# Head sums and means as float32r pairs, sample states as weights once, and a shorter lead, in a one-core hybrid decoder step

## The chip, the cores and the metric

The kernel runs on one core of a Trainium2 chip. The time is the device time of one execution in microseconds. Before the change, three runs took 1477.34, 1478.21 and 1481.64 us; the median is 1478.21.

A core has five engines that run side by side, each with its own instruction queue taken in order: TensorE (PE, matrix products; its weight loads are shown apart as PEld), VectorE (DVE), ScalarE (ACT), GpSimd (POOL) and SyncE (SP, which issues most of the transfers here). Products land in PSUM, in banks of 512 float32 columns; the other engines read them from there.

## The reference

One decoder layer runs for 512 prompt tokens and for 8 requests of 8 new tokens each, with shared weights; the kernel puts both beside each other as 576 columns. The layer is a half-step SwiGLU network, then three branches in parallel (an RWKV-7 recurrence, a causal convolution, attention to 256 memory tokens) that are gated and merged, then another SwiGLU network. The change touches three places of the recurrence. Cut down, they are:

```
s  = s * w_t + (s @ -kk_t) kka_t^T + v_t k_t^T ;  o_t = s @ r_t      # state per head, 64 x 64
mean = o.mean(-1);  var = square(o - mean).mean(-1)                  # per head of 64
o  = (o - mean) * rsqrt(var + GN_EPS) * gn_g + gn_b
o  = o + sum(r_h * k_h * r_k, -1) * v_h                              # head sum
```

The prompt starts with a state of zero; each of the 8 requests starts with its own state, an input. The new states are outputs.

## The kernel before

Data lie with channels on the 128 partitions and tokens along the columns, in halves of 288. A weight product in full precision is made of three float32r products: each operand is split into a high part (rounded to float32r, by a copy on ScalarE) and a low part (the rest, by a subtraction on VectorE), and high x high, high x low and low x high are added (`split`, L95; `mm3k`, L108). Smaller products outside the weight matrices are plain float32, which the instruction stream shows as two instructions each.

The program has a first SwiGLU network (to about 420 us), the mixing part (to about 985 us), the merge and the second network. The mixing part follows a written list of steps, `PLAN` (L28). For each of four pairs of heads there are `prep` (P: decays, keys, the 64-token products), `inverse` and `joined` (I, J: a triangular inverse, on VectorE and by transfers) and `chain` (B). The letters X, Y and Z are gate steps: large weight products that are independent of the chains.

The order on each engine is not the order of the text. A planner places instructions by its own estimate of when their data are ready, the earlier step of the program first, and so fills TensorE's gaps in a chain with weight products (L110) of later steps. A few products are pinned in program order (`busy` and parts of `chunks`). Once placed, the order on an engine is fixed.

*Head sums.* `prep` forms `k` = r k r_k on VectorE (L876). `full` (L122) multiplies it by `bd`, the 128 x 128 matrix with ones in the two 64 x 64 diagonal blocks, and L880 multiplies that sum by `v` to give `bv`.

*Chain.* `chain` transposes keys and values, runs `chunks` (L1041), eight steps of 64 prompt tokens that each need the state left by the one before, then `sample_chunk` (L1077) for the 64 sample tokens, then the normalisation. In `sample_chunk`, `ms` holds the 8 requests' states, loaded from `wst` by SyncE, as 128 x 128 blocks with two heads on the diagonal. They enter twice: L1086 lets them move against the weights `ax`, which hold request b's 8 columns of the decayed key and zeros elsewhere, and L1091 takes them as weights for the 8 columns of the receptance. L1098 to L1100 form the state's increment, with two buffers named "u2", and L1103 and L1104 update the states on VectorE before they are stored.

*Means.* L921 to L927 multiply the chain's output by `cen`, the identity minus the mean within a head, copy the result to `rs` and square it on ScalarE. Sums of squares, a root, a reciprocal and the rest follow; the last step of the fourth chain splits `ya` for the merge.

*Lead.* The program begins with 16 empty products on zeros (L207, `busy`), while the first half of the first slice of `x`, the vector table `pv`, and then slices of weights and of `x` by turns come in on SyncE's queue (L208 to L220).

Of the kernel before, what the change touches and what calls it, by code (L numbers as in the profile page):

```python
# [6 lines left out]
F32 = mybir.dt.float32  # L7
F32R = mybir.dt.float32r
AF = mybir.ActivationFunctionType
# [7 lines left out]
NB = 8  # L17
TS = 8
N = SEQ + NB * TS
H = N // 2  # L20
# [26 lines left out]
def _q8(t, q):  # L47
    return t.rearrange("p (b q) -> p b q", q=q)


class _Builder:
# [13 lines left out]
    def con(self, name, w=128):  # L65
        return self.cst[:, _CC[name]:_CC[name] + w]
# [107 lines left out]
    def build(self):  # L174
        tc, a = self.tc, self.a
        with ExitStack() as st:
# [19 lines left out]
            with ExitStack() as sf:  # L196
# [7 lines left out]
                x = [x1p.tile([128, N], F32, name=f"x{k}") for k in range(8)]  # L204
                idle = fp.tile([128, H], F32, name="m1")[:, :128]
                self.G.memset(idle, 0.0)
                self.busy(idle, idle, 16)  # L207
                self.dma(x[0][:, :H], a["x"][:, 0, :H])  # L208
                self.dma(self.pv, a["pv"])
                raw = []  # L210
# [3 lines left out]
                for k in range(8):  # L214
                    if k:
                        self.dma(x[k], a["x"][:, k, :])
                    self.dma(raw[k].rearrange("p (j c) -> p j c", j=3),
                             a["wu1"][:3, :, 128 * k:128 * (k + 1)].rearrange("j p c -> p j c"))
                    if not k:
                        self.dma(x[0][:, H:], a["x"][:, 0, H:])  # L220
                self.dma(self.cst, a["cst"])
# [3 lines left out]
                c = _COLS["mu"]  # L225
                self.V.tensor_scalar(self.omu, self.pv[:, c:c + 15], -1.0, 1.0, ALU.mult, ALU.add)
                c = _COLS["ka"]
# [22 lines left out]
            for step in PLAN.split():  # L250
                n = int(step[1:])
# [31 lines left out]
            x = [x2p.tile([128, N], F32, name=f"x2{k}") for k in range(8)]  # L283
# [321 lines left out]
    def lora(self, lp):  # L605
# [18 lines left out]
        self.ms = lp.tile([128, NB, 128], F32, name="ms")  # L624
        self.ax = lp.tile([128, 9, 64], F32, name="ax")
        for t in self.z:
            self.G.memset(t[:, 0:1], 0.0)
        self.G.memset(self.gi, 0.0)
        for t in self.padded(self.gi):
            self.G.memset(t[:, :, 0:1], 1.0)  # L630
        for t in self.st + [self.ms, self.ax]:
            self.G.memset(t, 0.0)
# [179 lines left out]
    def prep(self, j):  # L812
# [65 lines left out]
        bv = tmp("bv", 2)  # L878
        for c, p in self.full("g", (bd, k)):
            V.tensor_tensor(bv[:, c], p, v[:, c], ALU.mult)  # L880
# [17 lines left out]
    def chain(self, j):  # L898
# [21 lines left out]

        sq, rs = (b3.tile([128, 640], F32, name="u2", bufs=2)[:, :N] for _ in range(2))  # L921
        for c0, c1 in ((0, 5), (5, 9)):
            c = slice(64 * c0, 64 * c1)
            p = self.bank("c")[:, :64 * (c1 - c0)]
            T.matmul(_q8(p, 64), con("cen"), ra[:, c0:c1, 0, :], start=True, stop=True)
            A.copy(rs[:, c], p)
            A.activation(sq[:, c], rs[:, c], AF.Square)  # L927
        p = self.sums("c", [sq], con("bd")[:, ::64], slice(0, N))
# [148 lines left out]
    def sample_chunk(self, j, gr, kbt, vu, ra, gc):  # L1077
        V, A, T = self.V, self.A, self.T
        b3 = self.b3
        ms, ax = self.ms, self.ax  # L1080
        for h in range(2):
            s = slice(64 * h, 64 * h + 64)
            self.dma(ms[s, :, s], self.a["wst"][j, s])
        A.copy(_q8(ax.rearrange("p b t -> p (b t)"), 72)[:, :, :8], _q8(ra[:, 8, 1, :], 8))
        ps = self.values(8, gr, vu)
        self.solve(8, gr, vu, ps, [(ax[:, b, :], ms[:, b, :]) for b in range(NB)])  # L1086
        for h in range(2):
            s = slice(64 * h, 64 * h + 64)
            T.matmul(ps[s, 384:448], vu[:, 8, s], gr[:, h, 8, :64], start=True, stop=False)
        for b in range(NB):  # L1090
            T.matmul(ps[:, 384 + 8 * b:392 + 8 * b], ms[:, b, :], ra[:, 8, 0, 8 * b:8 * b + 8], start=False,  # L1091
                     stop=b == NB - 1)
        A.copy(ra[:, 8, 0, :], ps[:, 384:448])
# [169 lines left out]
```

## Time and profile before

| What | Value |
|---|---|
| Median of three runs | 1478.21 us |
| Profiled execution, its own time | 1475.84 us |
| Its span in the profile | 1474.1 us |
| TensorE busy | 1456.3 us (99%) |
| TensorE weight loads busy | 1376.0 us (93%) |
| VectorE busy | 1027.2 us (70%) |
| ScalarE busy | 674.3 us (46%) |
| HBM traffic | 97 GB/s over the span |

Products overlap in TensorE's pipeline and their ends are modelled, so a busy share of 99% does not say that every one runs at its peak pace. A line of a group reads: source line, engine, operation, output and inputs with shapes, count, then busy time and mean duration in ns, then idle time before it and what ended it. The chain of waits follows the work back from the last instruction, at each step to what released it. The granted clock is a share of TensorE's full clock.

### The profile page before, as it was taken

Reading aid. Unit: us, or ns where it says so; the run is one execution under the profiler, and the core shown is the slowest. Engines: PE = TensorE matmul, PEld = TensorE weight load, DVE = VectorE, ACT = ScalarE, POOL = GpSimd, SP = SyncE. Lnnn points to the kernel's source line nnn. Section 1 sums busy time; section 2 is a strip of 40 time slices with the busy share of each in tenths; the row PEclk is TensorE's granted clock in tenths of the full one; section 3 lists DMA queues with packets and bytes.
Section 4 is the critical chain, followed back from the end, with each engine's and each line's share of the span. In section 5 each row is a group of like instructions: output and inputs, shape, how many; then the busy total and the mean of one; then the engine's idle time right before and its main releaser. Section 6 shows DMA issues by size and latency. Waiting matters only on the chain.

```text
span 1474.1 us, 27109 instructions
## 1 busy us (share of the span) xinstructions
PE 1456.3 (99%) x10820; PEld 1376.0 (93%) x10820; DVE 1027.2 (70%) x2054; ACT 674.3 (46%) x1371; POOL 4.7 (0%) x22
## 2 busy tenths in 40 slices
PE   9999999999999999999999999999999999999998
PEld 9999999999999798889888888889999999999997
DVE  7976777777794579769456556357588667777765
ACT  7443434444577545435446543444354334344342
POOL 0000000000010000000000000000000000000000
PEclk9999999999999999999999999999999999999999
DMA  6222222223632144123223124355322322322221
GB/s 211 72 83 90 87 86 87 86 86 106 205 106 86 49 149 92 47 80 103 55 67 114 55 85 139 92 188 169 103 72 72 100 86 73 104 95 89 86 87 65
DMA packets 95178, 144.06 MB, mean 98 GB/s; under 512 B 43644, under 2 KB 53500, under 8 KB 95052
## 3 DMA queue, kind: packets, MB, share of 16 engines
q1 hardware_dynamic: 94476, 141.74, 31.5%
q8 instruction: 85, 1.39, 0.4%
q10 hardware_dynamic: 576, 0.59, 0.1%
q14 instruction: 41, 0.34, 0.1%
HBM read 126.07 MB, written 16.23 MB: 97 GB/s over the span
## 4 chain that ended last, share of the span: by engine, by line
PE 92%; DVE 4%; ACT 1%; DMA 1%; issue 1%; SPq 0%; DVEq 0%; ACTq 0%
PE p L110 51%; PE p L382 26%; PE c L1033 1%; PE g L893 1%; PE c L1037 1%; PE c L1023 1%; DVE pr L986 1%; PE c L128 1%; PE g L1056 1%; DVE cc L676 1%; PE g L128 1%; PE g L1054 1%; PE c L1050 1%; DMA w<-win 1%; PE c L1091 1%
## 5 line engine op out<-in xcount | busy, mean ns | idle before, releaser
L110 PE MATMUL p<-x,wh 128*128 128x288 f32 x3136 | 650.8, 299 | 1.4 <-ACT kv L562 0.7
L110 PEld LDWEIGHTS p<-x,wh 128*128 128x128 f32 x3136 | 504.4, 188 | 14.7 <-issue 7.4
L110 PE MATMUL p<-x,wl 128*128 128x288 f32 x1568 | 467.4, 298 | 2.3 <-DVE wl L97 2.1
L96 ACT CAST wh<-w 128x512 fp32r<-128x512 f32 (+1 forms) x353 | 209.9, 600 | 256.1 <-PE p L382 99.9
L97 DVE TENSOR_TENSOR wl<-w,wh 128x512 fp32r<-128x512 f32 (+1 forms) x353 | 232.0, 662 | 129.6 <-ACT wh L96 124.1
L110 PEld LDWEIGHTS p<-x,wl 128*128 128x128 f32 x1568 | 294.0, 188 | 7.1 <-DVE wl L97 2.7
L382 PE MATMUL p<-t,wh 128*128 128x288 f32 x1088 | 224.4, 299 | 0.0
L382 PEld LDWEIGHTS p<-t,wh 128*128 128x128 f32 x1088 | 173.8, 188 | 6.4 <-DVE t L393 6.4
L382 PE MATMUL p<-b,wh 128*128 128x288 f32 x816 | 169.7, 295 | 0.0
L382 PE MATMUL p<-t,wl 128*128 128x288 f32 x544 | 160.5, 295 | 0.0
L96 ACT CAST wh<-p 128x512 fp32r<-128x512 f32 x136 | 84.5, 621 | 155.9 <-PE p L110 117.3
L382 PEld LDWEIGHTS p<-b,wh 128*128 128x128 f32 x816 | 132.7, 188 | 0.0
L97 DVE TENSOR_TENSOR wl<-p,wh 128x512 fp32r<-128x512 f32 x136 | 93.7, 689 | 50.5 <-ACT wh L96 47.8
L382 PE MATMUL p<-b,wl 128*128 128x288 f32 x408 | 120.3, 295 | 0.0
L382 PEld LDWEIGHTS p<-t,wl 128*128 128x128 f32 x544 | 102.4, 188 | 0.0
L382 PEld LDWEIGHTS p<-b,wl 128*128 128x128 f32 x408 | 76.8, 188 | 0.0
L460 DVE SCALAR_TENSOR_TENSOR x<-p,x 128x288 f32<-128x288 f32 x128 | 57.9, 452 | 19.9 <-PE p L110 19.9
L96 ACT CAST x<-t 128x576 fp32r<-128x576 f32 (+1 forms) x60 | 36.5, 610 | 45.7 <-DVE t L464 42.5
L372 DVE TENSOR_TENSOR p<-w 128x512 f32<-128x512 f32 x68 | 46.7, 687 | 4.6 <-DMA w<-wu 4.2
L372 DVE TENSOR_TENSOR p<-p,w 128x512 f32<-128x512 f32 x68 | 46.5, 683 | 0.3 <-DMA w<-wu 0.2
L1067 DVE SCALAR_TENSOR_TENSOR st<-c,gc,mg 64x64 f32<-64x64 f32 x56 | 15.9, 283 | 42.8 <-PE c L1050 42.1
L676 DVE SCALAR_TENSOR_TENSOR cc<-up,pv,cc 128x512 f32<-128x512 f32 x60 | 43.5, 743 | 0.2
(354 smaller groups left out, 1979.4 us busy)
## 6 DMA issues: line engine op xcount, KB each, us to landing
w<-wu SPq DMA_DIRECT2D x85, 512.0 KB
w<-win SPq DMA_DIRECT2D x44, 512.0 KB
w<-wd SPq DMA_DIRECT2D x64, 256.0 KB
w<-wd SPq DMA_DIRECT2D x16, 384.0 KB
d_mb<-gate SPq DMA_DIRECT2D x16, 288.0 KB
w<-wo SPq DMA_DIRECT2D x8, 512.0 KB
d_x<-x SPq DMA_DIRECT2D x16, 144.0 KB
d_g<-gate SPq DMA_DIRECT2D x8, 288.0 KB
```

Source lines behind the costliest of these rows:

```text
L96: self.A.copy(hi, x)
L97: self.V.tensor_tensor(lo, x, hi.bitcast(F32), ALU.subtract)
L110: self.T.matmul(p, l, x[r][:, c], start=k == 0 and i == 0, stop=k == n - 1 and i == 2)
L128: self.T.matmul(p, l, r[:, c], start=i == 0, stop=i == len(ops) - 1)
L372: V.tensor_tensor(s, u, v, ALU.add)
L382: self.T.matmul(p, hl[l][:, c], xs[k][b][:, o], start=first and k == 0 and q == 0, stop=k == 3 and q == 2, skip_group_check=True)
L460: V.scalar_tensor_tensor(x[m][:, c], p, 0.5, x[m][:, c], ALU.mult, ALU.add)
L676: V.scalar_tensor_tensor(c[:, :SEQ], up[:, k:k + SEQ], w, c[:, :SEQ], ALU.mult, ALU.add)
L893: T.matmul(ps[:, i * 128:(i + 1) * 128], kb[o, c + i].rearrange("p a t -> p (a t)"), ra[o, c + i].rearrange("p a t -> p (a t)"), start=Tru ...
L986: V.tensor_tensor(pr, tt[:, :n, :e].unsqueeze(2).broadcast_to([np_, n, m, e]), l3[:, t:e, :e].unsqueeze(1).broadcast_to([np_, n, m, e]), A ...
L1023: p = self.T.matmul(ps[64:, 64 * h:64 * h + 64], gr[:64, h, c, 64:], vu[:64, c, 64 * h:64 * h + 64], start=h == 0 or alone, stop=alone)
L1067: V.scalar_tensor_tensor(mn[s, s], ps[s, 256 + 64 * h:320 + 64 * h], gc[s, c:c + 1], mg[s, s], ALU.mult, ALU.add)
```

## The change

- The head sums in `prep` become two float32r products: `k` is split into `kh` and `kl`, in the buffers "av" and "u1", and both are multiplied by `bdr`, a float32r copy of `bd`. The copy is exact, since the matrix holds ones and zeros.
- The centring in `chain` does the same with `cenr`, a float32r copy of `cen`, whose entries (63/64, -1/64 and 0) are exact too. The output is split into `yh` and `yl`, in "u2" buffers. Both banks are filled before they are copied to `rs`, and the square is one instruction over all columns. The two casts are made once, in `lora`.
- In `sample_chunk` the states are weights once: one product for each request moves 16 columns, 8 of the receptance and 8 of the key, into a bank "g" that is copied to `am`. Two identity products then add the halves where the old products added theirs. `ax` is gone.
- In the lead, 10 empty products stand in place of 16, and the first slice of weights is issued ahead of the first half of `x` and of `pv`.

```diff
-                self.busy(idle, idle, 16)
-                self.dma(x[0][:, :H], a["x"][:, 0, :H])
-                self.dma(self.pv, a["pv"])
+                self.busy(idle, idle, 10)
...
                     if not k:
+                        self.dma(x[0][:, :H], a["x"][:, 0, :H])
+                        self.dma(self.pv, a["pv"])
                         self.dma(x[0][:, H:], a["x"][:, 0, H:])
...
-        self.ax = lp.tile([128, 9, 64], F32, name="ax")
+        self.bdr, self.cenr = (lp.tile([128, 128], F32R, name=n) for n in ("bdr", "cenr"))
+        self.A.copy(self.bdr, self.con("bd"))
+        self.A.copy(self.cenr, self.con("cen"))
...
-        for c, p in self.full("g", (bd, k)):
+        kh = b1.tile([128, N], F32R, name="av")
+        kl = b1.tile([128, 640], F32R, name="u1", bufs=2)[:, :N]
+        self.split(kh, kl, k)
+        for c, p in self.full("g", (self.bdr, kh), (self.bdr, kl)):
...
-        sq, rs = (b3.tile([128, 640], F32, name="u2", bufs=2)[:, :N] for _ in range(2))
+        yh, yl = (b3.tile([128, 640], F32R, name="u2", bufs=2)[:, :N].rearrange("p (c t) -> p c t", t=64) for _ in "hl")
+        self.split(yh, yl, ra[:, :, 0, :])
+        cen = []
         for c0, c1 in ((0, 5), (5, 9)):
-            c = slice(64 * c0, 64 * c1)
-            p = self.bank("c")[:, :64 * (c1 - c0)]
-            T.matmul(_q8(p, 64), con("cen"), ra[:, c0:c1, 0, :], start=True, stop=True)
+            cen.append((slice(64 * c0, 64 * c1), self.bank("c")[:, :64 * (c1 - c0)]))
+            for i, y in enumerate((yh, yl)):
+                T.matmul(_q8(cen[-1][1], 64), self.cenr, y[:, c0:c1], start=i == 0, stop=i == 1)
+        rs = b3.tile([128, 640], F32, name="u2", bufs=2)[:, :N]
+        for c, p in cen:
             A.copy(rs[:, c], p)
-            A.activation(sq[:, c], rs[:, c], AF.Square)
+        sq = b3.tile([128, 640], F32, name="u2", bufs=2)[:, :N]
+        A.activation(sq, rs, AF.Square)
...
-        A.copy(_q8(ax.rearrange("p b t -> p (b t)"), 72)[:, :, :8], _q8(ra[:, 8, 1, :], 8))
+        q = self.bank("g")[:, :128].rearrange("p (b i t) -> p b i t", b=NB, i=2)
+        for b in range(NB):
+            T.matmul(q[:, b], ms[:, b, :], ra[:, 8, :, 8 * b:8 * b + 8], start=True, stop=True)
+        am = b3.tile([128, 2, 64], F32, name="am")
+        A.copy(am.rearrange("p i (b t) -> p b i t", t=8), q)
         ps = self.values(8, gr, vu)
-        self.solve(8, gr, vu, ps, [(ax[:, b, :], ms[:, b, :]) for b in range(NB)])
+        self.solve(8, gr, vu, ps, [(am[:, 1], ident)])
...
-        for b in range(NB):
-            T.matmul(ps[:, 384 + 8 * b:392 + 8 * b], ms[:, b, :], ra[:, 8, 0, 8 * b:8 * b + 8], start=False,
-                     stop=b == NB - 1)
+        T.matmul(ps[:, 384:448], ident, am[:, 0], start=False, stop=True)
```

More of the change, by code (lines that the diff above doesn't have):

```diff
@@ L630, in lora @@
             self.G.memset(t[:, :, 0:1], 1.0)
-        for t in self.st + [self.ms, self.ax]:
+        for t in self.st + [self.ms]:
             self.G.memset(t, 0.0)
@@ L1079, in sample_chunk @@
         b3 = self.b3
-        ms, ax = self.ms, self.ax
+        ms, ident = self.ms, self.con("ident")
         for h in range(2):
```

## The prediction

> **What bounds the kernel now.** I read the page first, then the stretch in which three of the four edits lie (440 to 985 us) by stages, then the chain of waits there. The page's first lines, and its line of shares of the chain that ended last:
>
> ```profile
> span 1474.1 us, 27109 instructions
> ...
> PE 1456.3 (99%) x10820; PEld 1376.0 (93%) x10820; DVE 1027.2 (70%) x2054; ACT 674.3 (46%) x1371; POOL 4.7 (0%) x22
> ...
> PE 92%; DVE 4%; ACT 1%; DMA 1%; issue 1%; SPq 0%; DVEq 0%; ACTq 0%
> ```
>
> TensorE carries 92% of that chain, so a product that goes is worth its own time unless something else is late behind it. Where something else is, the view by stages tells (stretch, its length, then the busy time of each engine, the granted clock, the DMA share):
>
> ```profile
> core 0: us, PE busy (x) PEld busy (x) DVE busy (x) ACT busy (x) POOL busy (x), PEclk, DMA share, GB/s
> ...
> 600.00:660.00 60.00, 60.00 (x422) 48.17 (x422) 39.18 (x89) 23.04 (x60) 0.00 (x0) 0.97 0.26 75
> 660.00:697.00 37.00, 34.89 (x240) 33.36 (x239) 36.00 (x74) 16.71 (x35) 0.00 (x0) 0.95 0.30 100
> 697.00:720.00 23.00, 22.39 (x212) 21.00 (x212) 14.14 (x33) 10.17 (x25) 0.00 (x0) 0.95 0.27 54
> ...
> 838.00:890.00 52.00, 52.00 (x372) 41.74 (x371) 25.94 (x73) 21.32 (x56) 0.00 (x0) 1.00 0.29 86
> 890.00:921.00 31.00, 28.54 (x254) 28.08 (x254) 19.31 (x39) 8.98 (x20) 0.00 (x0) 0.97 0.51 142
> 921.00:985.00 64.00, 63.84 (x439) 51.68 (x436) 25.84 (x54) 28.73 (x72) 0.00 (x0) 0.94 0.40 127
> ```
>
> The chains of the first, third and last head pair (600 to 660, 838 to 890, 921 to 985) leave TensorE no idle time: its gaps are filled with weight products of later steps. Between them stand stretches in which TensorE does idle: 660 to 697, where VectorE is busy 36.00 of 37.00 us with the convolution and the substitution of `inverse`, and 890 to 921, where TensorE waits 2.46 us for the end of another such substitution. There work on VectorE counts, and TensorE's does not.
>
> **The change part by part.** The tail of the third chain in the chain of waits (start, us, what), with the same steps of the first and the last chain where they took longer:
>
> ```profile
> 866.85 1.89 PE c L1033 x16
> ...
> 869.33 0.36 PE c L1033 x2
> ...
> 872.27 0.36 PE g L1056 x2
> ...
> 873.99 1.88 PE c L1091 x16
> ...
> 876.37 1.01 PE c L1100 x4
> 877.38 1.17 PE c L925 x4
> 878.54 0.66 PE p L110 x5
> ```
> ```profile
> 642.92 1.91 PE c L1100 x4
> 644.83 1.69 PE c L925 x4
> ...
> 963.52 1.90 PE c L1100 x4
> 965.42 1.82 PE c L925 x4
> ```
>
> *Samples' states.* A float32 product is two instructions. Before, the states pass twice: as moving data against `ax` (L1033, 16 instructions, 1.89 us) and as weights for `ra` (L1091, 16, 1.88 us). After, they are weights once, for 16 columns instead of 8. L1091 is paced by its weights (118 ns each whatever it moves, 1.88/16), so I give the new `q` products 1.88 us again. Two identity products come in: `am[:, 1]` as weights with 128 columns, the shape of L1033 x2 (0.36), and the identity as weights with 64 columns, the shape of L1056 x2 (0.36). Per head pair 1.88 + 0.36 + 0.36 - 1.89 - 1.88 = -1.17 us, over four -4.7. The copy `am` takes the place of the copy `ax` on ScalarE. `q` needs one of the two "g" banks, which the chunks' outputs use too; a wait for it would hold everything behind it on TensorE. Its cost lies between nothing (the chunks use one bank at a time) and the 1.88 us of its products once per chain; I take nothing.
>
> *Means.* L925 takes 1.17 us for 576 columns in float32. The float32r price comes from a run of weight products, and the float32 price of 288 columns, as in the head sums, from the convolution's mean, which has the same shape:
>
> ```profile
> 197.26 6.37 PE p L110 x48
> ...
> 777.49 1.94 PE g L128 x8
> ```
>
> One float32r product of 288 columns takes 6.37/48 = 0.133 us. The centring becomes high and low parts over 576 columns, as much as four of these: 0.53 us. That is -0.64 per head pair, -2.6 in all, without the slow first and last.
>
> *Head sums* (L880 with `full`). Four float32 instructions of 288 columns at 1.94/8 = 0.243 us become four float32r ones at 0.133: 0.97 - 0.53 = -0.44, over four -1.8.
>
> *What the halves cost.* Each split is a copy on ScalarE and a subtraction on VectorE:
>
> ```profile
> L96 ACT CAST x<-t 128x576 fp32r<-128x576 f32 (+1 forms) x60 | 36.5, 610 | 45.7 <-DVE t L464 42.5
> ```
> ```profile
> L97 DVE TENSOR_TENSOR cb0l<-cc,cb0h x1: 757/757/757, 796.0 to 796.0; 128x576 fp32r<-128x576 f32 x1
> ```
>
> Eight of each: 4.9 us on ScalarE, which is busy half of any stage above, and 6.1 on VectorE. The four of `k` lie behind L876, while TensorE makes the 48 products of `v` that bv waits for anyway (6.37 us by the row above): nothing. Without that cover each would cost 0.61 + 0.76. The four of the chain's output come at its tail. Those of the first and third chain push work into the two stretches where VectorE is late: 2 x 0.76 = +1.5. Bounds: 0 and 4 x 0.76 = 3.0. The two squares in one, and the casts of `bd` and `cen` made once at the start, stay on ScalarE beside other work: nothing.
>
> A new wait goes with the tail's split. Its buffers "u2" are held by `vx` until L1100 ends, and the subtraction stands on VectorE behind the update of the states, which L1100 releases too:
>
> ```profile
> 644.90 1.40 DVE L1103 TENSOR_TENSOR ms<-ms,c 64x512 f32<-64x512 f32 x2 [3.11 <-PE c L1100]
> 646.34 1.40 DVE L1104 TENSOR_TENSOR ms<-ms,gc 64x512 f32<-64x512 f32 x2
> ```
> ```profile
> 979.38 0.76 DVE L97 TENSOR_TENSOR u<-u,u 128x576 fp32r<-128x576 f32 x1 [0.74 <-ACT u L96]
> ...
> 985.46 0.40 PE L110 MATMUL p<-k,wh 128*128 128x288 f32 x1 [0.62 <-DVE gate L804]
> ```
>
> So the centring starts up to 1.40 + 1.40 + 0.76 = 3.56 us after L1100, where before it followed at once. What waits behind it is the chain's normalisation, and after that `ya`. In the last chain `ya` is done at 979.38 + 0.76 = 980.14 and first used at 985.46: 5.3 us of cover, of which 1.8 (1.17 + 0.64) go as TensorE's own work gets shorter; what is left, 3.5, just about covers the 3.56. In the others, later head pairs and gates fill. I take nothing, and keep the price for the rivals.
>
> *The lead.* Six empty products go, and the first weights are issued ahead of `x` and `pv`:
>
> ```profile
> 0.74 0.40 SPq L208 DMA_DIRECT2D x<-x  x1
> ...
> 0.99 5.34 PE L171 MATMUL p<-m 128*128 128x128 f32 x32 [0.99 <-POOL eps L223]
> ...
> 1.66 0.43 SPq L217 DMA_DIRECT2D w<-wu  x1
> ...
> 4.45 0.51 ACT L96 CAST t<-w 128x384 fp32r<-128x384 f32 x1 [0.71 <-DMA w<-wu]
> ```
> ```profile
> 7.24 0.78 ACT L422 ACTIVATE x<-x,pv 128x576 fp32r<-128x576 f32 x1 [1.25 <-DMA x<-x]
> ...
> 8.93 0.19 PEld L110 LDWEIGHTS p<-x,t 128*128 128x128 f32 x1 [0.26 <-DVE x L423]
> ...
> 9.39 0.19 PEld L110 LDWEIGHTS p<-x,t 128*128 128x128 f32 x1 [0.28 <-DVE t L97]
> ```
> ```profile
> 9.39 14.29 PE p L110 x106
> ```
>
> The empties end at 6.33 and the first slice's operands are there before. Twenty instructions at the mean 5.34/32 = 0.167 us end at 4.3, and the weights, issued at 0.74 instead of 1.66, come 0.9 us sooner, so the first 18 products start perhaps a microsecond earlier. But the second slice is what TensorE then waits for (0.26 and 0.28 us at 8.93 and 9.39), its `x` lands at 7.24, and its transfer stands behind the same bytes on the queue as before. From 9.39 on TensorE runs 106 products without a gap. So the lead gains nothing; bounds: -0.5 (both waits gone) and +0.9 (the 18 products at half the pace, another 18 x 0.133 = 2.4 us, less the 1 us won and the 0.54 idle).
>
> **Sum.** -4.7 - 2.6 - 1.8 + 1.5 = -7.6 us. The profiled execution took 1475.84 us, 1.7 around its span of 1474.1, and lies 2.4 below the median of the runs, 1478.21, and below the lowest. I carry the difference over: 1478.21 - 7.6 = 1470.6.
>
> **The rivals.** *The gain is hidden.* In the chain stretches the gaps between the serial steps are only stuffed with weight products. If the serial steps set the length, and stuffing runs out no later than now, what is taken from samples and means is given back as idle time, and only the head sums' -1.8 is left: 1476.4, no change. For it: TensorE idles 2.11 and 2.46 us in the two stages after a chain. Against: the chain of waits runs through the stuffing, all of which has to be done before 985. [...] I hold it to be less likely.
>
> *Slower: TensorE stands at the split.* TensorE takes its queue in order. Where the centring has been put in ahead of other ready products, all of them wait for the 3.56 us above. In all four chains this is +14.2: 1478.21 - 7.6 + 14.2 = 1484.8. It decides from the point where half of it shows (7.6/14.2); then the change is undone. For it: only five products, 0.66 us, stand between the centring and the sums now (row at 878.54). Against: many more are ready there.
>
> *More than the forecast.* In the first and last chain L1100 and L925 take 1.91 + 1.69 and 1.90 + 1.82 against 1.01 + 1.17 in the third. The granted clock (the first of the last three numbers; ahead of it length, busy time and count of TensorE) shows why:
>
> ```profile
> 643.00:644.00 1.00, 1.00 (x4) 0.50 0.73 284
> ...
> 764.00:765.00 1.00, 1.00 (x5) 1.00 0.00 0
> ```
>
> The clock halves for a few microseconds at 643 and not at 764 in the second chain, with TensorE busy in both, each time just behind the 16 products of 8 columns. These leave the tail now, so the halving may go with them: 0.90 + 0.52 + 0.89 + 0.65 = 3.0 us more. With VectorE's 1.5 hidden too: 1478.21 - 9.1 - 3.0 = 1466.1. [...]
>
> **How the numbers follow.** Forecast 0.55, hidden 0.18, slower 0.13, more 0.14. A measurement here tells about 0.3%, 4.4 us, from no change: 1473.8 to 1482.6. The forecast's own bounds run from 1478.21 - 9.1 - 0.5 = 1468.6 to 1478.21 - 7.6 + 1.5 + 0.9 + 1.9 (one wait for a bank) = 1474.9, so a little of it, 0.05, falls inside no change. Faster: 0.50 + 0.14 = 0.64. No change: 0.05 + 0.18 and 0.02 of the slower case half shown = 0.25. Slower: 0.11. The range, 1464.5 to 1481, holds the forecast, the hidden case and most of the larger gain, and leaves out most of the slower one.
>
> **What would show it.** Right: 64 instructions for `q` at about 118 ns, no L1091 blocks, centring x4 at about 0.53, head sums x4 at about 0.53; 600 to 985 shorter by about 7 us, and the lead still dense from about 9.4. Wrong: TensorE idle for more than 1 us ahead of the centring with VectorE as what ended it; more idle time in the two stages behind the chains; a clock at 0.5 where there was none; a lead that moves by more than 0.5 us.

## The result, and the profile after

The kernel got slower. Over 19 runs each the median is 1491.89 us after (1479.77 to 1503.77) and 1480.82 before (1476.42 to 1488.31); the ratio of the means is 1.0063, with a 95% interval of 1.0043 to 1.0082. The two slowest runs of the change, 1503.02 and 1503.77 us, lie over 1.5% above its fastest, count as slow and are left out of this ratio. The forecast was 1470.6, in a range to 1481.

The page after, in the three lines that answer to those of before:

```profile
span 1490.1 us, 26992 instructions
...
PE 1468.5 (99%) x10760; PEld 1384.8 (93%) x10760; DVE 1031.9 (69%) x2062; ACT 675.4 (45%) x1375; POOL 4.2 (0%) x21
...
PE 93%; DVE 4%; ACT 1%; issue 1%; DMA 1%; SPq 0%; DVEq 0%; ACTq 0%
```

TensorE has 60 instructions fewer and is busy 12.2 us longer; it idles 1490.1 - 1468.5 = 21.6 us instead of 17.8. So most of the 16.0 us by which the span grew is time in which the same products went slower. The view by stages (stretch, length, TensorE's busy time and instructions, granted clock, DMA share, GB/s) shows where, first of the kernel before and then of the one after:

```profile
520.00:560.00 40.00, 39.82 (x309) 1.00 0.46 138
...
725.00:790.00 65.00, 65.00 (x466) 1.00 0.25 75
790.00:850.00 60.00, 59.10 (x482) 1.00 0.28 76
```
```profile
520.00:560.00 40.00, 39.80 (x251) 0.83 0.38 122
...
725.00:790.00 65.00, 65.00 (x410) 0.87 0.23 67
790.00:850.00 60.00, 56.81 (x421) 0.89 0.26 77
```

At the same busy time, 58 products fewer pass in the first stretch. The granted clock is not low a little everywhere: the trace of either kernel has it at 1.00 or at 0.50, and 0.50 in single stretches. One of them in the kernel after, with the microsecond in which it begins and the one in which it ends:

```profile
540.00:541.00 1.00, 1.00 (x7) 0.55 0.76 133
...
550.00:551.00 1.00, 1.00 (x8) 0.83 0.00 0
```

With half clock inside, a mean of 0.55 puts the start at 540.10 and one of 0.83 the end at 550.34: 10.24 us. All half-clock stretches ahead of the last microseconds, in the profiles of before, of after, of e1 to e8 and of e10 to e12 below, last 3.41 us or a multiple of it (from 3.4 us, at 526 in the kernel after, to 17.1, at 841 in e1); this one is three times 3.41 us. A window below is such a 3.41 us, counted from where a half-clock stretch begins. Before, half clock adds up to 29.5 us over the whole span, after to 72.8.

All runs list time and mean granted clock. A line through 325 runs of the kernels below (one slope, a level for each kernel; runs of before that agree in both figures are taken once) falls by 1.25 us for each 0.001 of clock, and leaves 1.0 us of scatter. This splits each kernel's mean time into a part at equal clock and a part of the clock. Before, in the experiments' runs: mean 1482.7 at 0.9854. After, all 19 runs: 1491.7 at 0.9763, which is -2.5 at equal clock and +11.4 by the clock (-2.4 and +10.0 without the two slowest). The whole loss, and more, is clock. From the spread of the runs, a kernel's part by the clock below is uncertain by 0.7 to 2.4 us (one standard error) and its part at equal clock by about 0.5.

### The profile page after: what moved, and what is told of

Read it like the earlier page. It is cut to its first block, busy times and chain, and to the rows that moved or that the text cites. A ratio compares the mean times of both kernels' runs of the same rounds, so it can differ in the third digit from the quotient of the medians.

```text
span 1490.1 us, 26992 instructions
## 1 busy us (share of the span) xinstructions
PE 1468.5 (99%) x10760; PEld 1384.8 (93%) x10760; DVE 1031.9 (69%) x2062; ACT 675.4 (45%) x1375; POOL 4.2 (0%) x21
## 4 chain that ended last, share of the span: by engine, by line
PE 93%; DVE 4%; ACT 1%; issue 1%; DMA 1%; SPq 0%; DVEq 0%; ACTq 0%
PE p L110 53%; PE p L382 26%; PE g L898 1%; PE c L1047 1%; DVE pr L996 1%; PE c L1033 1%; PE c L1043 1%; PE c L128 1%; PE g L1066 1%; PE g L128 1%; DVE tt L998 1%; PE c L784 1%; PE g L1064 1%; PE g L138 1%; PE c L1060 1%
## 5 line engine op out<-in xcount | busy, mean ns | idle before, releaser
L110 PE MATMUL p<-x,wh 128*128 128x288 f32 x3136 | 659.7, 302 | 1.1 <-ACT kv L562 0.7
L110 PEld LDWEIGHTS p<-x,wh 128*128 128x128 f32 x3136 | 511.6, 190 | 17.5 <-issue 10.2
L96 ACT CAST wh<-w 128x512 fp32r<-128x512 f32 (+1 forms) x353 | 209.6, 600 | 257.3 <-PE p L382 99.2
L110 PEld LDWEIGHTS p<-x,wl 128*128 128x128 f32 x1568 | 297.8, 190 | 9.8 <-DVE wl L97 3.8
L96 ACT CAST wh<-p 128x512 fp32r<-128x512 f32 x136 | 84.5, 621 | 157.3 <-PE p L110 117.5
L96 ACT CAST x<-t 128x576 fp32r<-128x576 f32 (+1 forms) x60 | 36.5, 610 | 43.9 <-DVE t L464 40.7
```

Source lines behind the costliest of these rows:

```text
L96: self.A.copy(hi, x)
L110: self.T.matmul(p, l, x[r][:, c], start=k == 0 and i == 0, stop=k == n - 1 and i == 2)
```

## Experiments

In the labels, a head sum is `bv`'s product, a mean the centring. Head pairs and chains are numbered from 0, so pair 1 is the second; substitution 0 is pair 0's part of `inverse` on VectorE. Filler is what the planner puts into a gap of a chain: weight products of later steps. A quiet stretch is one in which few columns pass TensorE. All times are against runs of the kernel before on the same chip; "at equal clock" and "by the clock" are the two parts just named, in us against the mean of before.

| Kernel | Ratio (95%) | Mean clock | At equal clock | By the clock |
|---|---|---|---|---|
| the change | 1.0063 (1.0043 to 1.0082) | 0.9763 | -2.5 | +11.4 |
| e1 lead alone | 0.9984 (0.9957 to 1.0011) | 0.9853 | -1.6 | +0.1 |
| e2 sample states alone | 0.9993 (0.9968 to 1.0019) | 0.9847 | -0.2 | +0.8 |
| e3 means alone | 1.0038 (1.0006 to 1.0070) | 0.9823 | +2.2 | +3.9 |
| e4 head sums alone | 1.0079 (1.0049 to 1.0110) | 0.9790 | +5.0 | +8.0 |
| e5 head sums, pair 1 late | 1.0102 (1.0079 to 1.0125) | 0.9782 | +6.0 | +9.1 |
| e6 the change, pair 1 late | 0.9987 (0.9968 to 1.0005) | 0.9864 | -1.3 | -1.2 |
| e7 lead and sample states | 0.9991 (0.9969 to 1.0012) | 0.9847 | -2.6 | +0.9 |
| e8 means, split ahead of updates | 1.0024 (1.0003 to 1.0045) | 0.9875 | +5.6 | -2.6 |
| e10 the change, both of these | 0.9992 (0.9968 to 1.0016) | 0.9833 | -2.3 | +2.6 |
| e11 the change, 64 columns for `q` | 1.0021 (1.0004 to 1.0037) | 0.9807 | -2.2 | +5.9 |
| e12 e7 with head sums, pair 1 late | 1.0029 (1.0013 to 1.0046) | 0.9823 | +0.7 | +3.9 |
| e13 before, wide joining and attention | 1.0184 (1.0148 to 1.0221) | 0.9750 | +11.9 | +13.0 |
| e14 the change, the same | 1.0132 (1.0101 to 1.0162) | 0.9722 | +0.1 | +16.5 |
| e15 e6, the same and wide `q` | 1.0042 (1.0023 to 1.0062) | 0.9840 | +3.2 | +1.8 |
| e16 e7, the same | 1.0032 (1.0012 to 1.0052) | 0.9853 | +3.1 | +0.2 |
| e17 the change, wide attention alone | 0.9985 (0.9969 to 1.0002) | 0.9832 | -4.9 | +2.7 |
| e18 e6, wide attention alone | 1.0018 (0.9993 to 1.0043) | 0.9813 | -2.6 | +5.2 |

### The four parts, one at a time

Each kernel is the one before with one part of the diff. Where the matrix `bdr` or `cenr` is kept beside `ax`, the buffer `aux` is cut from 600 to the 576 columns that are used.

```diff
 e1: only the lead's lines of the diff
 e2: only sample_chunk's lines, and ax away
 e3: only the means' lines, and
-        aux = lp.tile([128, 600], F32, name="aux")
+        aux = lp.tile([128, 576], F32, name="aux")
 e4: only the head sums' lines, and aux as in e3
```

> The kernel before with the edit of the lead alone (10 empty products, first weights ahead of x and pv). The profile of the whole change loses 32.4 us of granted clock inside the program against 12.0 before (windows of 1 us, one minus the granted clock, summed up to the tail), and more idle time. Two theories of where that comes from. Quiet block: windows of about 3.4 us in which TensorE moves few columns are followed by windows at half clock, and the new products of 16 columns in the sample chunk are such a block; then this kernel is like before, median within 3 us, clock 0.985 to 0.99. Shifted plan: any edit moves the planner's order and so the quiet spots against the grid of windows; then this kernel loses too, 3 to 10 us, with a clock under 0.985, though no work after the first 10 us differs.

> The kernel before with the sample states as weights once, alone. Work by the prediction: -4.7 us. Quiet block: median 4 to 14 us above before and clock at or under 0.982, halvings right behind the 16 products of 16 columns in most chains. Shifted plan: anything from -5 to +8, with halvings at other places as often as there.

> The kernel before with the centring as two float32r products, alone (one idle auxiliary tile is 576 columns wide instead of 600 to make room). Work by the prediction: -2.6 us, +1.5 for VectorE. Quiet block: within 3 us of before, clock as before. Shifted plan: may lose 3 to 8 us.

> The kernel before with the head sums as two float32r products, alone (the auxiliary tile 576 columns wide). Work by the prediction: -1.8 us. Quiet block: within 3 us of before, clock as before. Shifted plan: may lose 3 to 8 us.

Lead and sample states alone make no difference that can be told; means and head sums alone each lose, the head sums most. So the sample states' products of few columns, which the first theory blamed, cost nothing by themselves: it falls as the cause in every chain (e11 below has what they do beside the other edits). "Shifted plan" is not borne out for the lead. The clock's parts of the four (0.1 + 0.8 + 3.9 + 8.0 = 12.8) come near the whole's 11.4, within their uncertainty; the parts at equal clock (+5.4 in all) don't come near the whole's -2.5.

The 5.0 us that the head sums lose at equal clock stand in e4's profile as idle time. Its span is 19.1 us longer than that of before. TensorE idles 22.1 us instead of 17.8, which is 4.3 of them. Half clock lasts 60.0 us instead of 29.5, which is 15.3 if it costs half of its time, and -0.5 is left for the products. The new idle time is spread over short waits, the longest 1.88 us at 823 for a cast of weights on ScalarE (L96).

### Pair 1 kept late

With the head sums alone the planner starts pair 1's `prep` early: its scan and the reciprocal behind it run at 548 to 554 us, in the middle of pair 0's substitution on VectorE, which now ends at 572.4 instead of 555.2. The change has the same order. The views in time order, of before and of e4 (start, us, then the instruction; the last `TENSOR_REDUCE` ends the substitution):

```profile
554.66 0.50 DVE L988 TENSOR_REDUCE tt<-pr 108x11 f32<-108x352 f32 x1
570.43 1.37 DVE L833 TENSOR_TENSOR_SCAN g<-w,gi 128x592 f32<-128x592 f32 x1
```
```profile
548.32 1.38 DVE L835 TENSOR_TENSOR_SCAN g<-w,gi 128x592 f32<-128x592 f32 x1
...
571.86 0.55 DVE L993 TENSOR_REDUCE tt<-pr 108x11 f32<-108x352 f32 x1
```

To take that order away, pair 1's first gate tile is put into a buffer that the substitution reads:

```diff
-        sg = b1.tile([128, 640], F32, name="u1", bufs=2)[:, :N]
+        if j == 1:
+            sg = b1.tile([128, 1024], F32, name="lt")[:, :N]
+        else:
+            sg = b1.tile([128, 640], F32, name="u1", bufs=2)[:, :N]
```

> The head sums alone, as in the run before, and one more edit: the first gate tile of pair 1's prep lies in the buffer that substitution 0 reads, so that pair 1's first products, scan and reciprocal can't be placed inside substitution 0 (the order on VectorE has them behind it again, as in the kernel before). 'Early pair': the loss of 12 us came from that order, which stretched substitution 0 by 10 us and left the attention products of 538 to 552 us without filler, so that they fell to half clock; then substitution 0 ends at 554 +-2 us, there is no half clock from 538 to 552, and the ratio to the kernel before is 0.997 to 1.002. 'Own work': the splits themselves and what waits for them in the preps cost it; then the ratio stays at 1.005 to 1.011.

> The whole change with the same extra edit (pair 1's first gate tile in the buffer that substitution 0 reads). 'Early pair': the ratio falls from 1.0063 to 0.996 to 1.002 and the mean clock rises from 0.976 to about 0.985. 'Own work': it stays at 1.004 to 1.009. If it falls only half way (1.002 to 1.004), the means' part (1.0038 alone) is what is left.

The order came back in both; in e5 (first) and e6 the substitution ends with

```profile
561.86 0.50 DVE L996 TENSOR_REDUCE tt<-pr 108x11 f32<-108x352 f32 x1
```
```profile
560.28 0.52 DVE L1001 TENSOR_REDUCE tt<-pr 108x11 f32<-108x352 f32 x1
```

For the whole change the loss is gone (0.9987), at the same operations: what the change lost was not the price of its operations. For the head sums alone it stayed (1.0102, inside "own work"). So "early pair", as a cause that works wherever it stands, falls: the early order is not enough to explain the loss, and taking it away does not always mend it. In both, part of the half clock at 538 to 552 us stayed (0.76 there in e5 and e6, 0.53 in e4, 1.00 before).

### Lead with sample states, and the means' wait

e7 is the diff's lead and `sample_chunk` lines together. e8 is e3 with the updates of `ms` moved into a function that is called behind the split:

```diff
-        self.sample_chunk(j, gr, kbt, vu, ra, gc)
+        ps = self.sample_chunk(j, gr, kbt, vu, ra, gc)
...
         self.split(yh, yl, ra[:, :, 0, :])
+        self.update(j, gc, ps)
```

> The lead and the sample states alone, without head sums and means. 'Adds up': the two ratios measured alone (0.9984 and 0.9993) give 0.998, 1480 us beside 1483.5, and at equal clock the work is 4 to 6 us less. 'Lost to the clock': every saving of work in the chains turns into quiet windows, and the ratio is 1.000 or above.

> The means alone, with the updates of the sample states written behind the split instead of ahead of it, so that the split's subtraction doesn't stand behind them on VectorE. 'Wait': the stretch from the copy of the samples' output to the root falls from 8.1 us to 4 to 5.5 us, the ends of chains 2 and 3 come 3 to 7 us earlier than with the means alone, and the ratio falls from 1.0038 to 0.998 to 1.001. 'Clock alone': the stretch gets shorter but the ratio stays at 1.002 to 1.006, since the loss was half-clock windows that lie where they lie by chance.

e7 is faster by 2.6 us at equal clock, and not to be told from before in its ratio: neither side's number came in. In e8 the wait is real and goes. From the copy of the samples' output to the root in the second chain, where neither has half clock, in e3 and in e8:

```profile
763.20 0.21 ACT L1100 COPY ra<-c 128x64 f32<-128x64 f32 x1 [2.61 <-PE c L1098]
772.42 0.27 ACT L937 ACTIVATE rt<-c,eps 128x10 f32<-128x10 f32 x1
```
```profile
760.38 0.21 ACT L1101 COPY ra<-c 128x64 f32<-128x64 f32 x1 [2.62 <-PE c L1099]
767.27 0.27 ACT L938 ACTIVATE rt<-c,eps 128x10 f32<-128x10 f32 x1
```

9.2 us become 6.9: 2.3 less, within the 3.56 that the prediction gave as the most. (In the other chains 10.3 to 11.0 become 6.6 to 6.9, but there e3 has 3.4 to 5.4 us of half clock in the stretch and e8 none.) The ratio only went from 1.0038 to 1.0024, and at equal clock the kernel is not faster (+5.6 against +2.2): in its profile TensorE idles 23.1 us against 20.3 in e3's, the longest new wait 2.53 us at 918 for a cast of weights (L96). So a chain's tail that gets shorter does not by itself shorten the kernel.

### The clock by itself

A block of empty products stands ahead of everything else, so that nothing else is on TensorE. The helper is this, with `xr` a float32r copy of a slice of `x`, `xf` the slice itself and `xz` zeros (both float32):

```diff
+        def ck_run(t, n, count, rows=128, cols=128):
+            for _ in range(count):
+                tc.keep_in_program_order(self.T.matmul(pk[:cols, :n], t[:rows, :cols], t[:rows, :n],
+                                                       start=True, stop=True))
```

> The kernel before with a block of empty products in front of everything else, whose results nobody reads: runs of 300 float32r products on one slice of x that move 128, 96, 64, 48, 32 and 16 columns, each between runs of 180 that move 288; then 16, 32, 64, 96, 128, 192 and 288 columns without such runs between; zeros instead of x; 64 rows; 64 columns of weights; plain float32 with 64 columns; and eight bursts of 24 products of 16 columns between 110 of 288. The time is longer by the block and says nothing; the granted clock in each run is what is read. 'Array use': the clock is decided by how many columns pass in a window of 3.41 us; from the six traces so far the border is at about 2,900 columns a window (0.85 columns per ns), so the runs of 16 to 64 columns go at 0.5, 128 and up at 1.0, 96 lies near the border, no idle time is needed, and in the rising runs the clock stays at 0.5 up to a wider product than in the falling ones. 'Idle': the clock is halved only after TensorE stood idle; then all runs without gaps go at 1.0, whatever they move.

The stretches of the block (columns as above):

```profile
32.00:62.00 30.00, 30.00 (x271) 1.00 0.00 1
...
94.00:146.00 52.00, 52.00 (x246) 0.50 0.00 1
...
774.00:836.00 62.00, 62.00 (x293) 0.50 0.00 1
844.00:872.00 28.00, 28.00 (x253) 1.00 0.01 1
962.00:994.00 32.00, 32.00 (x289) 1.00 0.00 1
...
1132.00:1164.00 32.00, 32.00 (x290) 1.00 0.00 1
1188.00:1206.00 18.00, 18.00 (x143) 1.00 0.00 1
```

They are, in order: 128 columns, coming from full clock; 96 columns, coming from full clock; 128 columns, coming from half clock; 192 columns, behind these; zeros with 64 float32 columns; `xf` with 64 float32 columns; the first burst of 16 columns with 288 around it. This is one execution. TensorE has no idle time in any of the stretches, so "idle" falls for this block and "array use" fits it. Worked out from the counts, the columns that pass in 3.41 us are 271/30 x 128 x 3.41 = 3,940 in the first stretch, at 1.00 throughout. At the same pace 96 columns give 2,960, and the clock goes to 0.50 at 91.9 us, 4 us after they begin. At 0.50 a product of 128 columns takes 62/293 = 0.212 us instead of 30/271 = 0.111; that makes 2,060 columns a window, and the clock stays at 0.50 for all 62 us. Behind them 192 columns, 3,090 a window at the same 0.212 us, bring it back to 1.00 at 842.9. An estimate from these four: one border at about 3,000 columns per 3.41 us, between 2,960 and 3,090, fits them all. Since the same products passed at about half the rate at 0.50, a stream that had held full clock did not win it back: 128 columns stand at 1.00 or at 0.50 depending on what came before. Sixty-four float32 columns are 290/32 x 64 x 3.41 = 1,980 by count and stayed at 1.00, so by this estimate a float32 column counts for more than one; zeros stayed at 1.00 at the same pace (289 in 32 us). The bursts of 24 products of 16 columns, 2.6 us, brought no halving in any of eight; each straddled the edge of two windows, if the windows counted from the earlier half clock are carried on, and so by the estimate left over 3,000 columns in both.

With this estimate the window at 540 can be read. The groups of TensorE's products in the 3.41 us ahead of it, in the kernel after (the first three rows) and the kernel before:

```profile
L784 PE MATMUL c<-pts,vc 128*128 128x16 f32 x18 | 2.3, 268 | 0.0
L128 PE MATMUL g<-la,wda 64*128 64x288 f32 x3 | 1.1, 437 | 0.0
L775 PE MATMUL c<-cst,s 128*128 128x128 f32 x2 | 0.4, 286 | 0.2 <-DVE s L772 0.2
```
```profile
L110 PE MATMUL p<-x,wh 128*128 128x288 f32 x8 | 1.7, 304 | 0.0
L782 PE MATMUL c<-pts,vc 128*128 128x16 f32 x13 | 1.5, 256 | 0.0
L110 PE MATMUL p<-x,wl 128*128 128x288 f32 x5 | 1.5, 292 | 0.0
```

Before, 13 weight products of 288 columns stand between the attention products of the samples: 3,740 columns from these alone. After, none does; `prep`'s product for pair 1 stands there instead, on 64 of 128 rows. The columns of the three rows are 18 x 16 + 3 x 288 + 2 x 128 = 1,408, all float32. Counted at 3,000/1,980 = 1.5 each, the least that the block allows, they make 2,110, and counted double 2,820: under 3,000 both ways.

The kernels' own profiles fit the estimate. Of their 7,968 windows at full clock (nineteen profiles, all but the block's), 149 are followed by half clock. With a float32 column counted as two and a product under part of the array by its share of 128 x 128, both chosen because they fit, a border of 2,800 columns names 122 of the 149, and 8 others; in the profiles of before and after alone, 14 of 16 and 2 others. By this count a joining product further down, 32 float32 columns under 32 x 32 weights, comes to 32 x 2/16 = 4 columns.

### The change in both ways, and the head sums beside others

e10 is e6 with e8's move; e11 the change with 64 columns in the product of each request's states, of which two copies pick the 16 wanted; e12 the change without the means and with pair 1 late.

```diff
 e11:
-            T.matmul(q[:, b], ms[:, b, :], ra[:, 8, :, 8 * b:8 * b + 8], start=True, stop=True)
+            o = 32 * (b // 4)
+            T.matmul(q[:, 64 * b:64 * b + 64].rearrange("p (i t) -> p i t", i=2), ms[:, b, :], ra[:, 8, :, o:o + 32],
+                     start=True, stop=True)
```

> The whole change, with pair 1's first gate tile in the buffer that substitution 0 reads, and with the updates of the sample states written behind the split of the means. 'Adds up': the updates' wait (chain 3's output 2.3 us earlier in work, from 973.2 to 970.9 when the means stood alone) and the freed order of pair 1 add, so the ratio goes from 0.9987 to 0.995 to 0.998. 'Plan by plan': each order has its own quiet windows, the gains don't add, and the ratio lies anywhere from 0.997 to 1.008, with the time following the mean clock at 1.3 us per 0.001.

> The whole change, but the product of each request's states moves 64 columns instead of 16 (the 16 wanted ones among them; two copies pick these), at a weight load that takes as long as before. Pair 1 still starts early. 'Array use': the half-clock windows that follow these products in chains 1 and 3 (765 to 772 and 977 to 984 us of the profile after) go or get shorter, those of 526 to 605 us stay, and the ratio falls from 1.0063 to 1.001 to 1.005. 'Elsewhere': these products are too short to decide a window, and the ratio stays at 1.004 to 1.008.

> The change without the means: lead, sample states and head sums, with pair 1's first gate tile in the buffer that substitution 0 reads. 'Own work': the head sums cost work wherever they stand (with the same tile edit they cost 1.0 per cent alone); the ratio is 1.004 to 1.012. 'Plan by plan': beside lead and sample states the head sums cost about nothing, and the ratio is 0.995 to 1.002.

e10: the gains don't add; "plan by plan" holds. e11: the windows behind `q` went, at the same work, and the ratio came where "array use" had it. So beside the other edits `q` did lead into half clock. Of the change and of e11:

```profile
765.00:772.00 7.00, 7.00 (x27) 0.53 0.01 2
977.00:984.00 7.00, 7.00 (x28) 0.51 0.00 0
```
```profile
765.00:772.00 7.00, 7.00 (x48) 1.00 0.00 0
977.00:984.00 7.00, 6.96 (x47) 1.00 0.45 115
```

The planner moved other instructions too, so the columns are not the only difference: the half clock between 526 and 605 us, which was to stay, went from 17.1 to 10.2 us, and 13.7 us of it came at 847. e12 (1.0029) lies between the two expectations: head sums cost something beside lead and sample states, at equal clock 0.7 + 2.6 = 3.3 against e7 (with pair 1 moved as well), but less than alone.

### Wider quiet products

The same on two other groups of products: those that join the halves of the inverse (32 columns become 64), and the samples' attention (16 become 64, a few 48). In e13 to e16 both, in e17 and e18 the attention alone; the columns added are overwritten or never read.

```diff
 attention:
-                        T.matmul(po[:, j, 4 * g + b, :16], vc[:, m, 128 * j:128 * j + 128], pts[:, c:c + 16],
-                                 start=m == 0, stop=m == 1)
+                        n = (64, 64, 64 - 16 * j, 16)[b]
+                        o = 256 * j + 128 * g + 32 * b
+                        T.matmul(pf[:, o:o + n], vc[:, m, 128 * j:128 * j + 128], pts[:, c:c + n],
+                                 start=m == 0, stop=m == 1)
 joining, the first of two:
-                T.matmul(ps[96:128, h, c, :], gr[64:96, h, c, 96:128], t1[:, h, c, :], start=True, stop=True)
+                n = 32 if h and c == 7 else 64
+                o = 256 * h + 32 * c
+                T.matmul(pf[96:128, o:o + n], gr[64:96, h, c, 96:128], tf[:, 288 * h + 32 * c:288 * h + 32 * c + n],
+                         start=True, stop=True)
```

> The kernel before, with two groups of quiet products made wider by columns that nobody reads: the joining products move 64 columns instead of 32, the attention products of the samples 64 (a few 48 or 16) instead of 16. The block alone showed that a plain float32 instruction with 64 columns takes 0.112 us, as one with 16 does (0.108). 'Columns decide': the half-clock windows behind the joining of pairs 1 and 3 (717 to 724 and 919 to 926 us before) go or get shorter, the mean clock rises from 0.985 to 0.988 or more, and the ratio is 0.994 to 0.998. 'Companion': the clock stays at 0.983 to 0.987 and the ratio at 0.999 to 1.004 (the planner counts the wider products and moves others).

> The changed kernel with the same wider joining and attention products; pair 1 still starts early. 'Columns decide': the half clock of 540 to 550 us goes or is halved, those behind the joinings too, the mean clock rises from 0.976 to 0.982 or more, and the ratio falls from 1.0063 to 0.998 to 1.003. 'Companion': the clock stays below 0.979 and the ratio above 1.004.

> The changed kernel with pair 1's first gate tile in the buffer that substitution 0 reads, the wider joining and attention products, and 64 columns in the product of each request's states. 'Columns decide': the clock rises from 0.986 to 0.989 or more, and at 2 us less work than before the ratio is 0.993 to 0.997, faster than both kernels. 'Companion': as with the late start alone, 0.997 to 1.001.

> Lead and sample states alone, with the wider joining and attention products. 'Columns decide': the clock rises from 0.985 to 0.988 or more, and the ratio falls from 0.9991 to 0.993 to 0.997, faster than both kernels. 'Companion': it stays at 0.997 to 1.002.

All four came out slower than "columns decide" had them, three of them (e13, e15, e16) slower than either theory. The premise was wrong for the joining products: their weights are 32 x 32, and they had taken 1.19/32 = 0.037 us each, not 0.11. A second group of 32 before and in e13, both at full clock:

```profile
714.68 1.19 PE L1016 MATMUL c<-gr,aux 32*32 32x32 f32 x32 [0.28 <-ACT aux L1011]
```
```profile
713.85 1.92 PE L1027 MATMUL c<-gr,aux 32*32 32x64 f32 x32
```

1.19 us became 1.92, and in e13 and e14 half clock came between 560 and 600 us, where the first joining is (a mean of 0.91 in both, 1.00 before and in the change). The 540 window of the change had gone in e14, though, as expected (1.00 from 540 to 550). So the attention was tried alone:

> The changed kernel with wider attention products alone (64 columns, a few 48 or 16, instead of 16), joining products as they were. Pair 1 still starts early. 'Columns decide': 540 to 550 us goes at full clock (0.51 before this edit), the new half-clock windows at the first joining (582 to 589 us with both widened) go too, and the ratio falls from 1.0063 to 0.999 to 1.004. 'Any widening costs': the planner's other order costs what it cost with both widened, and the ratio is 1.008 to 1.015.

> The changed kernel with pair 1's first gate tile in the buffer that substitution 0 reads, and the wider attention products. 'Columns decide': the half clock of 538 to 545 us goes, the clock is 0.987 to 0.991, and the ratio is 0.994 to 0.998. 'Any widening costs': 1.002 to 1.006, as with the joining and request products widened too.

In e17 the ratio fell from 1.0063 to 0.9985, with intervals that don't touch, and nothing was taken out. The stretch that answers to the window at 540, the groups of TensorE's products in the same 3.41 us ahead of 540.10 (the two costliest of five), and pair 1's scan on VectorE:

```profile
540.00:550.00 10.00, 10.00 (x79) 1.00 0.21 69
```
```profile
L787 PE MATMUL c<-pts,vc 128*128 128x64 f32 x20 | 2.4, 277 | 0.0
L110 PE MATMUL p<-x,wh 128*128 128x288 f32 x3 | 0.8, 321 | 0.0
```
```profile
543.73 1.37 DVE L838 TENSOR_TENSOR_SCAN g<-w,gi 128x592 f32<-128x592 f32 x1
```

Seventy-nine products pass at full clock; counted as above, the wide products and four of 288 columns make over 3,000. Of the half clock at the first joining one window is left, at 582 (a mean of 0.83 from 580 to 590). Pair 1 still starts early in e17, in the middle of substitution 0, which ends at 563.3 (571.2 in the change).

So the early order does not cost by itself: with it, and with the stretch at 540 filled, the loss is gone. How much of the gain is that stretch's own is open. Ahead of the last microseconds half clock went from 64.9 to 37.5 us, by eight windows. Four of them stood behind attention products (at 526 and 540); the other four are the balance of places where the edit changed nothing but the order. At equal clock e17 is 2.4 us faster than the change as well. In e18 the half clock at 538 to 545 went as well, but other windows came behind it:

```profile
538.00:545.00 7.00, 7.00 (x58) 1.00 0.43 142
...
780.00:792.00 12.00, 12.00 (x52) 0.57 0.07 26
968.00:984.00 16.00, 16.00 (x86) 0.68 0.16 45
```

Its ratio, 1.0018, is neither theory's. With columns added, quiet stretches went at full clock: at 540 in e14 and e17, at 538 in e18 and behind `q` in e11 (1.00 each). That a kernel gets faster by it is not shown: everything behind is placed anew by the planner, and in e18 other stretches fell to half clock (the means of 0.57 and 0.68 above). No kernel here beats the kernel before by more than its interval.

## Why the prediction was wrong

The step that failed is one that the sum does not contain: it priced every product by its duration before and so took the granted clock, and the order that the planner makes, as given. "The four of `k` ... nothing" and "I take nothing" for the waits were judged by cover, and cover is filler; which filler stands where is what the edit changed. The clock was named under the third rival, but only as a gain of 3.0, and was given no price on the slower side. It cost 11.4 us on the mean. A second term was too small: the waits that the halves bring were put at +1.5, and the profile after has 3.8 us more idle time.

Point by point:

*Sample states, -4.7.* Right in size where it was made. `q` and the two identity products, from the third chain after:

```profile
886.92 1.75 PE g L1097 x16
...
889.16 0.36 PE c L1043 x2
...
891.75 0.36 PE c L1105 x2
```

`q` is 1.75 us (0.109 each, forecast 0.118), the identities are 0.36 each, no block like L1091 is left, and no bank was waited for. But alone it is worth 0.2 us at equal clock; 1.7 us more idle time in e2's profile are part of the difference, the rest is open.

*Means, -2.6.* The price of a product was about right: the two of 320 and two of 256 columns of a chain take 0.51 to 0.73 us, forecast 0.53. The wait was there, and where the prediction put it; the first chain after:

```profile
651.91 1.40 DVE L1116 TENSOR_TENSOR ms<-ms,c 64x512 f32<-64x512 f32 x2 [0.89 <-PE c L1113]
653.34 1.40 DVE L1117 TENSOR_TENSOR ms<-ms,gc 64x512 f32<-64x512 f32 x2
654.78 0.76 DVE L97 TENSOR_TENSOR u<-ra,u 128x576 fp32r<-128x576 f32 x1
```

TensorE did not stand at it; the view of the tile `cenr` gives all the idle time before its products (what ended it: us, times):

```profile
  DVE u L97: 0.3, 1
```

So the slower rival, as it was put, did not happen. The means alone still lost 2.2 us at equal clock, in place of a gain of 2.6; in their profile TensorE idles 2.5 us longer than before.

*Head sums, -1.8.* The four products do take 0.53 us: starts 0.13 apart in the last pair.

```profile
845.75 0.29 PE L128 MATMUL g<-av,bdr 128*128 128x288 f32 x1
...
846.15 0.29 PE L128 MATMUL g<-u,bdr 128*128 128x288 f32 x1
```

Alone they cost 5.0 us at equal clock and 8.0 by the clock. The 5.0 is idle time, as e4's profile showed, where the prediction had taken "nothing" for what the halves cost. Which operations bring these waits is not settled: the same edit beside lead and sample states cost 3.3, and in the whole change the parts at equal clock come to less than nothing.

*Lead, 0 (-0.5 to +0.9).* Missed by a little. TensorE runs without a gap from 6.03 instead of 9.39, and the sums at the end of the first run start at 22.87 instead of 23.68, in the chain of waits after and before:

```profile
6.03 16.84 PE p L110 x125
22.87 1.01 PE p L138 x10
```
```profile
23.68 1.01 PE p L138 x10
```

That is -0.8 us, outside the bound of -0.5; alone the lead gave -1.6 at equal clock. The second slice's wait went, which the prediction had taken as fixed by the bytes on the queue.

*The sum.* In the profiled execution, half-clock time grew by 43.3 us. If half clock costs half of it, that is 21.7 us; by the slope of the runs (1.25 us for 0.001 of 1,480) it is 18.3. Idle time grew by 3.8. The span grew by 16.0, so 6 to 9.5 us of TensorE's work went: near the 4.7 + 2.6 + 1.8 = 9.1 that the sum took from TensorE. The +1.5 for VectorE's late stretches did not come where it was put: in the one behind the first chain TensorE waits 1.89 us instead of 2.11, behind the third 1.60 instead of 2.45. The 3.8 us of idle time stand elsewhere, the longest 2.14 us at 824, for a copy on ScalarE (L857). The savings that the prediction counted were there; the half clock that it did not count was twice as large.

*The rivals.* "The gain is hidden" had the part at equal clock better than the forecast did: -2.5 against its -1.8 and the forecast's -7.6. Some of the gain was given back as idle time, as it says, but not in the two stages that it named.

## What to carry to other kernels

Before pricing an edit at its operations' durations, add up how many columns TensorE moves in each 3.41 us around it: in the block of e9 the clock went to 0.50 without any idle time at about 2,960 float32r columns per 3.41 us, held 1.00 at 3,940, and came back at about 3,090 passed at half the rate. A float32 instruction that moves 16 columns under 128 x 128 weights took as long here as one that moves 64 (0.109 and 0.110 us), so the quiet stretch at 540 could be filled in the same time; whether the kernel gains by it must be run (e17 did, e18 did not). And where a planner sets the order, test each part alone and in company: the parts of this change did not add up, and moving one tile to another buffer took back the whole loss.

## What the hardware showed that was not expected

- The same stream of products, 128 columns each, ran for 33 us at a clock of 1.00 (0.111 us each) and for 62 us at 0.50 (0.212 us each), depending on what came before it. In the kernels half clock lasted for up to five windows in a row in the profiles listed above (17.1 us at 841 in e1).
- The run-to-run spread of the changed kernel is almost all clock: the change's 19 runs go from 1479.77 to 1503.77 us as their mean clock goes from 0.985 to 0.966, and time and clock are correlated at -0.996. From profile to profile the half-clock stretches lie at other phases of 3.41 us (one begins at 526.46 in the change and one at 538.82 in e4, 3.6 windows later). That the phase also differs between two executions of one program and makes the spread is a guess: no program was profiled twice.
- A plain float32 instruction with 64 columns took as long as one with 16 when its weights were 128 x 128 (0.110 us at 290 in 32 us, against 1.75/16 = 0.109), but not with 32 x 32 weights, where 32 instructions of 32 columns took 1.19 us and of mostly 64 columns 1.92.
